# Modulation products of four column groups moved into the DeltaNet chain

## The chip, the cores and the metric

The kernel runs on one core of a Trainium2 chip. The metric is the device time of one execution in microseconds (us). Engines: TensorE (PE in the profile; its weight loads are PEld), VectorE (DVE), ScalarE (ACT), GpSimd (POOL) and SyncE (SP), whose queue here issues nearly all DMAs.

## The reference

One inference step of a hybrid backbone with two layers, over 512 latent tokens (`x_sample`) and 128 context tokens (`x_prompt`). Cut to what matters here:

```python
def trunk_layer(x, cond, ...):
    mod = (jax.nn.silu(cond) @ w_ada + b_ada)[:, None, :]
    shift1, scale1, gate1, shift2, scale2, gate2 = jnp.split(mod, 6, axis=-1)
    h = rmsnorm(x, norm1_g) * (1 + scale1) + shift1
    q, k, v, z, dn_a, dn_b, u_ssm, u_pool, gates = jnp.split(h @ w_in, offsets, axis=-1)
    o_dn, st_dn = deltanet_mixer(q, k, v, z, ...)      # chunked, in both directions
    o_ssm, st_re, st_im = s5_mixer(u_ssm, ...)         # complex diagonal scan, in both directions
    o_pool = pool_mixer(u_pool, pool_w, pool_scale)
    g_dn, g_ssm, g_pool = jnp.split(jax.nn.sigmoid(gates), N_BRANCH, axis=-1)
    merged = g_dn * (o_dn @ w_branch_dn) + g_ssm * (o_ssm @ w_branch_ssm) + g_pool * (o_pool @ w_branch_pool)
    x = x + gate1 * (merged @ w_out)
    h = rmsnorm(x, norm2_g) * (1 + scale2) + shift2
    x = x + gate2 * conv_ffn(h, ffn_w_up, ffn_conv, ffn_w_down)
```

`w_ada` is 1024 x 6144 in float32 for each layer; `cond` is one vector for the latent and one for the context tokens, so the modulation is a product of two rows with 25 MB of weights a layer. It depends on nothing but `cond`: it can be computed at any time before it is used.

## The kernel before

All activations stand transposed, 128 channels on the partitions and the 640 tokens along the free dimension, and a product of a weight tile with them (`mm3`, lines 377 to 389) is made of three float32r products, high and low parts, in two halves of 320 columns. Its accumulator is one of two `acc` tiles in PSUM. A weight tile is loaded by SP's queue into one of four raw buffers (`wraw`, tag of four), and split into a high part by ScalarE (L235) and a low part by VectorE (L372). Such a tile of 1024 input rows is 48 products, L384, L386 and L388.

**The modulation** is computed in column groups of 2048: group 0 is shift1 and scale1, group 1 gate1 and shift2, group 2 scale2 and gate2. `ada_pieces` gives a group as nine entries. Eight are pieces, one for each 128 rows of `w_ada`: two loads of 128 x 1024 (`wada`, L443), which take two of the same four raw buffers, and four products of 512 columns in 32-column tiles of the array (L446), which the profile counts as eight instructions. All eight pieces accumulate in one small PSUM tile; `sm` has four. The ninth entry transposes the row (L456) and adds the bias into `mods[l]`.

**The order of the work** comes from two sources. A layer runs, one after another: a state-space chain (`s5_chain`, with the branch that ends in the glu and `w_branch_ssm` tiles, here called the state-space output stretch), the DeltaNet chain, the projections, and the FFN. The chains are generators that yield an estimate of how much other work fits beside each step; a queue of other work, `Weave`, is stepped while it has credit from these estimates, times `wv.scale`. `extra` entries are put between the tiles of the queue; in the FFN, `ffn_extra` is called once a tile. The list that comes out so is then handed to a planner, which reorders the instructions of each engine by its own costs and readiness and takes the list order as priority, so that a later entry whose operands are there can be issued before an earlier one.

In the DeltaNet chain the queue holds the last four q/k/v tiles and the eight gate tiles (`gate`, stored to `g_dram`); `wv.drain(12)` runs it down to twelve entries ahead of the chain. The chain itself: `start` (transposes of K and V to DRAM), `ahead` and `dn_diag` (L1363, L1365, L1414), `dn_inverse` (L1463 to L1511), `dn_step` (L1552 to L1593), `finish` (L1876); nearly all of its products go to `sm` tiles, which VectorE or ScalarE read out. K, V and P are loaded back by SP's queue (L1532, L1533, L1542).

Group 0 of layer 0 is computed at the kernel's head by a function of its own. Group 1 of layer 0 stands among the tiles of the state-space chain of layer 0 and stays there. The other four groups stand as follows: group 2 of each layer among the tiles of its state-space output stretch, groups 0 and 1 of layer 1 in the FFN of layer 0.

Of the kernel before, what the change touches and what calls it, by code (L numbers as in the profile page):

```python
# [259 lines left out]
def hybrid_dit_kernel(ctx: ExitStack, tc: tile.TileContext, a, outs, depth=DEPTH, taps=None):  # L260
# [171 lines left out]
    def ada_pieces(l, p, mod, grp, E=None):  # L432

        box = {}

        def rows_k(k):
            if k == 0:
                box["ps"] = sm()
            ps = box["ps"]
            for hf in range(2):  # L440
                t = E() if E else wpool.tile([P, 1024], F32, name="wada", tag="wraw", bufs=WRAW)
                c0 = grp * 2048 + hf * 1024
                nc.sync.dma_start(t, a["w_ada"][l, k * P:(k + 1) * P, c0:c0 + 1024])  # L443
                for j in range(2):
                    q = 32 * (2 * hf + j)
                    PE.matmul(ps[q:q + 32, :], silu_c[:, k, :], t[:, j * 512:(j + 1) * 512],  # L446
                              start=k == 0, stop=k == KT - 1, tile_position=(0, q))
            if k == KT - 1:
                box["row"] = row = ar.take(512)
                S.activation(row.f, ps, AF.Copy)  # L450

        def finish():
            row = box["row"]
            pt = sm()
            for b in range(4):
                PE.transpose(pt[:, b * P:(b + 1) * P], row.f[:, b * P:(b + 1) * P], ident)  # L456
            row.free()

            src = pt.rearrange("p (b j r) -> p r j b", b=4, j=4)[:, 0:2]
            dst = mod[:, :, grp * 16:(grp + 1) * 16].rearrange("p s (j b) -> p s j b", j=4)  # L460
            bias = p["b_ada"][:, grp * 16:(grp + 1) * 16].rearrange("p (j b) -> p j b", j=4)
            for st in range(2):
                V.tensor_tensor(dst[:, st], src[:, st], bias, op=OP.add)

        return [(1.7, lambda k=k: rows_k(k)) for k in range(KT)] + [(0.6, finish)]
# [1165 lines left out]
        V.tensor_mul(y.f, y.f, sq.f)  # L1631
        sq.free()

    def layer(l, xs, p, qf, mod, wv, extra, ffn_extra, begin, nxt):

# [15 lines left out]
        def store(dr, i, t):  # L1653
            nc.sync.dma_start(dr[i], t.f)
            t.free()

        def gate(w):

            ps = acc()
            mm3(ps, w, hs)  # L1660
            g_ = ar.take(NT)
            S.activation(hv(g_.f), ps[:, :, :HF], AF.Tanh, scale=0.5)
            return g_

        def gate_w(n, m):
            return lambda: Stream(w_in, OFF_G + n * D, D).tile(m)
# [86 lines left out]
        def kq(m):  # L1753
            return tile_of(qkv, m, w_in, 0)
# [16 lines left out]
        extra = deque(extra)  # L1771
# [11 lines left out]
        work = [tile_of(glu, m, a["ssm_glu_w"][l], 0, 4) for m in range(4)]  # L1783
        for m in range(KT):
            work += gated(1, a["w_branch_ssm"][l], oS, m)
        extra.extend(ada_pieces(l, p, mod, 2))
        for w in work:
            wv.add(*w)
            if extra:
# [4 lines left out]
        qT, kT = ys[0:4], ys[4:8]  # L1794
        for m in range(8, 12):
            wv.add(*kq(m))
        for m in range(KT):
            wv.add(6.5, lambda w, m=m: store(g_dram, m, gate(w)), gate_w(0, m))
        wv.add(0.0, lambda: free_pairs(hb))


        def norms():
# [83 lines left out]
        tk = {}  # L1886
        with ln_exp():
            wv.run(together(deltanet_ab(l, hs, w_in, tk), norms()))
            wv.drain(12)
        vT = ys[8:12]  # L1890
        with tc.issue_after(last_rsq[0].ins):
            for t in vT:
                silu2(t)
        wv.run(one_by_one(start(), ahead(0, 3)))
        wv.run(together(inverse(0, 3), ahead(1, 2, 4)))
        wv.scale = 0.4
        wv.run(together(inverse(1, 2), inverse(4), steps((0, 0)), steps((1, 3))))
        wv.scale = 0.6
        wv.run(together(steps((0, 1), (0, 2), (0, 3)), steps((1, 2), (1, 1), (1, 0))))
        wv.scale = 1.0  # L1900
        wv.run(together(steps((0, 4)), steps((1, 4)), finish(2), finish(1)))
# [7 lines left out]
        first = []  # L1909
# [175 lines left out]
    wv = Weave(ar)  # L2085
    for l in range(depth):
        first = ada_pieces(0, ps_[0], mods[0], 1) if l == 0 else ()
        extra = deque()
        if l + 1 < depth:
            ps_.append({})  # L2090
            lps, lds = [], []
            kept = []
            extra.append(lambda: (kept.append(s5_kept()), lps.append(load_params(l + 1, GP))))
            extra.extend([lambda: None] * 4)
            extra.append(lambda: ps_[l + 1].update(params(l + 1, lps[0])))
            for grp in range(2):
                extra.extend(f for _, f in ada_pieces(l + 1, ps_[l + 1], mods[l + 1], grp))
            extra.extend([lambda: None] * (60 - len(extra)))
            extra.insert(60, lambda: lds.append(s5_load(l + 1, GP, kept[0])))
            extra.insert(64, lambda: qs.append(s5_params(lds[0])))  # L2100
        qf = (lambda: s5_params(ld0)) if l == 0 else lambda: qs[0]

        def nxt():
            w_in = a["w_in"][l + 1]
            ws = [wraw(w_in, OFF_SSM + m * P, KT, P) for m in range(2)]
            return scales(mods[l + 1], 8, ps_[l + 1]["norm1"]), mods[l + 1][:, :, 0:8], ws

        done = layer(l, xs, ps_[l], qf, mods[l], wv, first, extra, begin, nxt if l + 1 < depth else None)
        if done:
            xs, begin = done  # L2110

# [30 lines left out]
```

## Time and profile before

| | us |
|---|---|
| median of three runs | 2593.4 (2589.87 to 2594.01) |
| the profiled execution's own time | 2591.93 |
| its span, first to last instruction | 2590.2 |
| mean granted TensorE clock (1 is 2.4 GHz) | 0.973 |

| stretch, from the trace | us from the start |
|---|---|
| state-space output stretch, layer 0 / layer 1 | 390 to 520 / 1660 to 1790 |
| DeltaNet chain, layer 0 / layer 1 | 570 to 770 / 1830 to 2030 |
| FFN of layer 0 | 860 to 1330 |

The profile gives for each engine the time in which it was busy. A wait is put down to the instruction whose signal came last. Busy times of one engine in a stretch are compared with the length of the stretch: an engine that is busy all the time bounds it.

### The profile page before, as it was taken

The page shows a single profiled execution, that of the slowest core. Times are in us where ns is not written, and L with a number is a line of the kernel's source. Part 1 is how long each engine was busy: PE and PEld are TensorE (multiplying, and loading weights), DVE is VectorE, ACT ScalarE, POOL GpSimd, SP SyncE. Part 2 cuts the span into 40 slices and gives each one's busy share as a digit, 9 for nine tenths or more (in the row PEclk, how much of TensorE's full clock was granted, in tenths as well). Part 3 has the DMA queues.
Part 4 walks back from the last instruction along what each step waited for, and adds up shares of the span by engine and source line. Part 5 has one row for each costly group of instructions (what it writes and reads, how often), then busy time and mean ns, then how long its engine had stood idle before and what let it go on. Part 6 is the DMA issues. An engine that isn't in the chain of part 4 may idle for free. (4 is left out here: it accounts for less than half of the span.)

```text
span 2590.2 us, 43654 instructions
## 1 busy us (share of the span) xinstructions
PE 2440.7 (94%) x17225; PEld 2321.6 (90%) x17225; DVE 1608.3 (62%) x3250; ACT 989.8 (38%) x1792; POOL 555.2 (21%) x560
## 2 busy tenths in 40 slices
PE   7899989998889999999988999899989999999999
PEld 6688987997789988999988998799879899999998
DVE  5768863269866743553596687633897766445355
ACT  4242342363333531442443423424533354334243
POOL 3521320135342100000134404311445320000000
PEclk8899999999889999999999999999999999999999
DMA  9833327344253255322237232463454322222221
GB/s 309 162 112 94 91 64 233 114 127 140 94 178 95 74 172 178 98 67 81 75 115 103 59 113 79 118 197 99 138 166 160 112 66 74 74 74 78 78 66 66
DMA packets 382016, 297.29 MB, mean 115 GB/s; under 512 B 33706, under 2 KB 336500, under 8 KB 381812
## 3 DMA queue, kind: packets, MB, share of 16 engines
q1 hardware_dynamic: 377892, 286.53, 38.4%
q0 software_dynamic: 3552, 7.73, 1.2%
q8 instruction: 136, 2.23, 0.4%
q14 instruction: 68, 0.56, 0.1%
q10 hardware_dynamic: 368, 0.25, 0.0%
HBM read 251.45 MB, written 42.48 MB: 113 GB/s over the span
## 5 line engine op out<-in xcount | busy, mean ns | idle before, releaser
L384 PE MATMUL acc<-pg,whi 128*128 128x320 f32 x4064 | 943.2, 313 | 5.9 <-ACT pg L235 2.9
L388 PE MATMUL acc<-pg,wlo 128*128 128x320 f32 x4064 | 936.0, 311 | 8.0 <-DVE wlo L372 8.0
L386 PE MATMUL acc<-pg,whi 128*128 128x320 f32 x4064 | 938.0, 311 | 4.9 <-DVE pg L411 4.9
L372 DVE TENSOR_TENSOR wlo<-wraw,whi 128x512 fp32r<-128x512 f32 (+1 forms) x538 | 414.5, 776 | 524.3 <-ACT whi L235 518.1
L384 PEld LDWEIGHTS acc<-pg,whi 128*128 128x128 f32 x4064 | 681.4, 189 | 47.1 <-issue 16.7
L388 PEld LDWEIGHTS acc<-pg,wlo 128*128 128x128 f32 x4064 | 684.5, 189 | 10.5 <-DVE wlo L372 8.9
L386 PEld LDWEIGHTS acc<-pg,whi 128*128 128x128 f32 x4064 | 685.4, 189 | 6.0 <-DVE pg L411 5.4
L235 ACT ACTIVATE whi<-wraw 128x512 fp32r<-128x512 f32 (+1 forms) x538 | 331.7, 623 | 925.4 <-PE acc L386 723.0
L235 ACT ACTIVATE pg<-pg 128x640 f32<-128x640 f32 (+8 forms) x335 | 222.0, 682 | 262.5 <-DVE pg L1996 56.1
L235 ACT ACTIVATE pg<-sm 128x512 f32<-128x512 f32 (+9 forms) x245 | 109.5, 470 | 207.1 <-PE sm L1502 59.4
L235 ACT ACTIVATE pg<-acc 128x640 f32<-128x640 f32 (+3 forms) x196 | 127.0, 655 | 73.9 <-PE acc L388 49.5
L700 DVE SCALAR_TENSOR_TENSOR pg<-pg,cols_f 128x511 f32<-128x511 f32 (+1 forms) x130 | 65.9, 548 | 49.8 <-ACT pg L235 49.7
L411 DVE TENSOR_TENSOR pg<-pg,pg 128x640 fp32r<-128x640 f32 x84 | 68.6, 821 | 41.4 <-ACT pg L235 37.6
L713 POOL DMA_DIRECT2D pg<-in_ssm_lambda_re_dram x2 | 1.2, 583 | 407.9 <-ACT whi L235 407.9
L1685 POOL TENSOR_TENSOR pg<-pg,pg 128x640 f32<-128x640 f32 x21 | 38.9, 1855 | 226.1 <-DVE pg L1683 146.9
L691 DVE SCALAR_TENSOR_TENSOR pg<-acc,mod,pg 128x320 f32<-128x320 f32 x56 | 30.8, 549 | 78.3 <-PE acc L388 78.2
L235 ACT ACTIVATE pg<-acc,cols_f 128x640 f32<-128x640 f32 (+1 forms) x88 | 68.3, 776 | 0.0
L701 DVE SCALAR_TENSOR_TENSOR pg<-pg,cols_h 128x511 f32<-128x511 f32 (+1 forms) x130 | 65.6, 546 | 0.0
L446 PE MATMUL sm<-wada,silu_c 128*32 128x512 f32 x320 | 57.9, 627 | 8.0 <-DMA wada<-in_w_ada_dram 8.0
L1683 DVE SCALAR_TENSOR_TENSOR pg<-pg,acc 128x640 f32<-128x640 f32 x48 | 39.0, 817 | 40.9 <-PE acc L388 35.3
L906 POOL TENSOR_TENSOR pg<-pg,pg 128x512 f32<-128x512 f32 (+1 forms) x32 | 54.7, 1710 | 1.9
L901 POOL TENSOR_TENSOR pg<-s_cp,pg 128x640 f32<-128x640 f32 x16 | 27.6, 1725 | 127.4 <-PE acc L388 55.8
(392 smaller groups left out, 2960.8 us busy)
## 6 DMA issues: line engine op xcount, KB each, us to landing
wraw<-in_w_in_dram SPq DMA_DIRECT2D x96, 512.0 KB, 4.4
wraw<-in_ffn_w_up_dram SPq DMA_DIRECT2D x88, 512.0 KB, 3.9
wada<-in_w_ada_dram SPq DMA_DIRECT2D x80, 512.0 KB, 4.4
wraw<-in_ffn_w_down_dram SPq DMA_DIRECT2D x32, 512.0 KB, 3.9
mg_dram<-pg SPq DMA_DIRECT2D x32, 320.0 KB, 2.2
pg<-mg_dram SPq DMA_DIRECT2D x32, 320.0 KB, 5.2
wraw<-in_w_out_dram SPq DMA_DIRECT2D x16, 512.0 KB, 3.9
pg<-in_w_ada_dram SPq DMA_DIRECT2D x6, 1024.0 KB, 10.8
```

The lines of the kernel that those rows point to most:

```text
L235: ins = self.engine.activation(out, in_, func, **kw)
L372: V.tensor_sub(lo, src, hi)
L384: PE.matmul(ps[:M, h, :HF], hi[:, k, :M], hh[:, h * HF:(h + 1) * HF], start=first and k == 0, stop=False)
L386: PE.matmul(ps[:M, h, :HF], hi[:, k, :M], hl[:, h * HF:(h + 1) * HF], start=False, stop=False)
L388: PE.matmul(ps[:M, h, :HF], lo[:, k, :M], hh[:, h * HF:(h + 1) * HF], start=False, stop=last and k == n - 1)
L411: V.tensor_sub(lo.r, src, hi.r)
L446: PE.matmul(ps[q:q + 32, :], silu_c[:, k, :], t[:, j * 512:(j + 1) * 512], start=k == 0, stop=k == KT - 1, tile_position=(0, q))
L700: V.scalar_tensor_tensor(y[:, b + 1:e], r[:, b:e - 1], w0, y[:, b + 1:e], op0=OP.mult, op1=OP.add)
L701: V.scalar_tensor_tensor(y[:, b:e - 1], r[:, b + 1:e], w2, y[:, b:e - 1], op0=OP.mult, op1=OP.add)
L906: E.tensor_tensor(oo, oo, t.f, op=OP.add if r else OP.subtract)
L1683: V.scalar_tensor_tensor(hv(g_.f), hv(g_.f), 1.0, ps[:, :, :HF], op0=OP.add, op1=OP.mult)
L1685: GP.tensor_tensor(g_.f, g_.f, mg.f, op=OP.add)
```

## The change

The four groups leave their places and become entries of the queue of the DeltaNet chain, between the gate tiles: three entries behind the first, two behind each of the others, the rest behind the eighth. Layer 0's chain gets group 2 of layer 0, the parameter transposes of layer 1 and group 0 of layer 1; layer 1's chain gets groups 2 and 1 of layer 1. The loads of layer 1's parameters go from the FFN of layer 0 to its state-space chain in the list. `drain` runs the queue down to the number of entries that were added from the gates on, and two of the chain's scales are raised, 0.4 to 0.5 and 0.6 to 0.75. Nothing that is computed changes.

```diff
--- before.py
+++ after.py
@@ -1631,7 +1631,7 @@
         V.tensor_mul(y.f, y.f, sq.f)
         sq.free()
 
-    def layer(l, xs, p, qf, mod, wv, extra, ffn_extra, begin, nxt):
+    def layer(l, xs, p, qf, mod, wv, extra, late, ffn_extra, begin, nxt):
 
 
 
@@ -1783,7 +1783,6 @@
         work = [tile_of(glu, m, a["ssm_glu_w"][l], 0, 4) for m in range(4)]
         for m in range(KT):
             work += gated(1, a["w_branch_ssm"][l], oS, m)
-        extra.extend(ada_pieces(l, p, mod, 2))
         for w in work:
             wv.add(*w)
             if extra:
@@ -1794,9 +1793,17 @@
         qT, kT = ys[0:4], ys[4:8]
         for m in range(8, 12):
             wv.add(*kq(m))
+        before = len(wv.q)
+        late = deque([*ada_pieces(l, p, mod, 2), *late])
         for m in range(KT):
             wv.add(6.5, lambda w, m=m: store(g_dram, m, gate(w)), gate_w(0, m))
+            for _ in range(2 if m else 3):
+                if late:
+                    wv.add(*late.popleft())
         wv.add(0.0, lambda: free_pairs(hb))
+        for w in late:
+            wv.add(*w)
+        after_v = len(wv.q) - before
 
 
         def norms():
@@ -1886,16 +1893,16 @@
         tk = {}
         with ln_exp():
             wv.run(together(deltanet_ab(l, hs, w_in, tk), norms()))
-            wv.drain(12)
+            wv.drain(after_v)
         vT = ys[8:12]
         with tc.issue_after(last_rsq[0].ins):
             for t in vT:
                 silu2(t)
         wv.run(one_by_one(start(), ahead(0, 3)))
         wv.run(together(inverse(0, 3), ahead(1, 2, 4)))
-        wv.scale = 0.4
+        wv.scale = 0.5
         wv.run(together(inverse(1, 2), inverse(4), steps((0, 0)), steps((1, 3))))
-        wv.scale = 0.6
+        wv.scale = 0.75
         wv.run(together(steps((0, 1), (0, 2), (0, 3)), steps((1, 2), (1, 1), (1, 0))))
         wv.scale = 1.0
         wv.run(together(steps((0, 4)), steps((1, 4)), finish(2), finish(1)))
@@ -2085,16 +2092,16 @@
     wv = Weave(ar)
     for l in range(depth):
         first = ada_pieces(0, ps_[0], mods[0], 1) if l == 0 else ()
+        late = ada_pieces(l, ps_[l], mods[l], 1) if l else []
         extra = deque()
         if l + 1 < depth:
             ps_.append({})
             lps, lds = [], []
             kept = []
-            extra.append(lambda: (kept.append(s5_kept()), lps.append(load_params(l + 1, GP))))
-            extra.extend([lambda: None] * 4)
-            extra.append(lambda: ps_[l + 1].update(params(l + 1, lps[0])))
-            for grp in range(2):
-                extra.extend(f for _, f in ada_pieces(l + 1, ps_[l + 1], mods[l + 1], grp))
+            first = [*first, (0.0, lambda: lps.append(load_params(l + 1, GP)))]
+            late.append((0.6, lambda: ps_[l + 1].update(params(l + 1, lps[0]))))
+            late.extend(ada_pieces(l + 1, ps_[l + 1], mods[l + 1], 0))
+            extra.append(lambda: kept.append(s5_kept()))
             extra.extend([lambda: None] * (60 - len(extra)))
             extra.insert(60, lambda: lds.append(s5_load(l + 1, GP, kept[0])))
             extra.insert(64, lambda: qs.append(s5_params(lds[0])))
@@ -2105,7 +2112,7 @@
             ws = [wraw(w_in, OFF_SSM + m * P, KT, P) for m in range(2)]
             return scales(mods[l + 1], 8, ps_[l + 1]["norm1"]), mods[l + 1][:, :, 0:8], ws
 
-        done = layer(l, xs, ps_[l], qf, mods[l], wv, first, extra, begin, nxt if l + 1 < depth else None)
+        done = layer(l, xs, ps_[l], qf, mods[l], wv, first, late, extra, begin, nxt if l + 1 < depth else None)
         if done:
             xs, begin = done
 
```

## Rows read from the trace of the kernel before

**Rows 1.** The page: engines' busy time (share) and TensorE's forty slices, in tenths.

```profile
PE 2440.7 (94%) x17225; PEld 2321.6 (90%) x17225; DVE 1608.3 (62%) x3250; ACT 989.8 (38%) x1792; POOL 555.2 (21%) x560
...
PE   7899989998889999999988999899989999999999
```

**Rows 2.** Busy time by stretch, all engines; columns in the first line.

```profile
core 0: us, PE busy (x) PEld busy (x) DVE busy (x) ACT busy (x) POOL busy (x), PEclk, DMA share, GB/s
390.00:450.00 60.00, 60.00 (x366) 45.96 (x365) 20.67 (x32) 17.31 (x28) 3.13 (x2) 1.00 0.75 240
570.00:645.00 75.00, 64.60 (x433) 62.97 (x431) 69.80 (x117) 29.48 (x60) 39.06 (x34) 0.93 0.44 140
645.00:770.00 125.00, 104.79 (x813) 97.20 (x814) 92.57 (x198) 41.53 (x107) 52.92 (x44) 0.88 0.41 135
940.00:1040.00 100.00, 100.00 (x684) 88.63 (x683) 39.80 (x79) 27.00 (x45) 0.00 (x0) 1.00 0.61 182
1830.00:1930.00 100.00, 87.84 (x594) 84.92 (x594) 91.24 (x163) 47.61 (x102) 45.71 (x41) 0.95 0.49 155
1930.00:2030.00 100.00, 88.23 (x791) 82.66 (x790) 79.32 (x164) 34.99 (x85) 51.27 (x42) 1.00 0.46 157
```

**Rows 3.** Timeline of TensorE, FFN of layer 0: start us, length us, what.

```profile
941.08 0.46 PE L386 MATMUL acc<-pg,whi 128*128 128x320 f32 x2
941.38 0.46 PE L388 MATMUL acc<-pg,wlo 128*128 128x320 f32 x2
941.77 1.06 PE L446 MATMUL sm<-wada,silu_c 128*32 128x512 f32 x8
...
943.16 0.46 PE L386 MATMUL acc<-pg,whi 128*128 128x320 f32 x2
...
966.10 0.46 PE L388 MATMUL acc<-pg,wlo 128*128 128x320 f32 x2
966.40 0.60 PE L456 MATMUL sm<-cst,pg 128*128 128x128 f32 x4
...
967.13 0.46 PE L386 MATMUL acc<-pg,whi 128*128 128x320 f32 x2
```

**Rows 4.** Timeline of TensorE, output stretch of layer 0: half a piece.

```profile
408.91 1.05 PE L446 MATMUL sm<-wada,silu_c 128*32 128x512 f32 x4
```

**Rows 5.** Busy time of line 446 alone, output stretches of layers 0 and 1.

```profile
390.00:450.00 60.00, 14.55 (x64) 2.12 (x64) 1.00 0.75 240
1660.00:1725.00 65.00, 12.88 (x64) 1.84 (x64) 0.95 0.67 213
```

**Rows 6.** Timeline of TensorE and VectorE, head of layer 1's output stretch.

```profile
1663.70 1.92 PE L446 MATMUL sm<-wada,silu_c 128*32 128x512 f32 x16
1669.45 1.92 PE L446 MATMUL sm<-wada,silu_c 128*32 128x512 f32 x4 [3.83 <-DMA wada<-in_w_ada_dram]
1671.64 1.92 PE L446 MATMUL sm<-wada,silu_c 128*32 128x512 f32 x4 [0.26 <-DMA wada<-in_w_ada_dram]
1673.49 0.64 PE L384 MATMUL acc<-pg,whi 128*128 128x320 f32 x1
...
1668.15 0.69 DVE L372 TENSOR_TENSOR wlo<-wraw,whi 128x512 fp32r<-128x512 f32 x1 [0.80 <-ACT whi L235]
```

**Rows 7.** TensorE's waits, chain of layer 0: total us, times, longest us.

```profile
PE sm L1463 <- DVE pg L1457: 9.1, 3, 6.4
PE sm L1414 <- ACT pg L235: 7.5, 3, 3.3
PE acc L405 <- ACT pg L235: 4.4, 2, 4.2
```

**Rows 8.** Instructions of line 317, the parameter loads; first and last start last.

```profile
L317 POOL DMA_DIRECT2D rows_a<-in_b_ada_dram x1: 535/535/535, 61.0 to 61.0; - x1
```

**Rows 9.** Waits of SP's queue, chain of layer 0: total us, times, longest us.

```profile
SPq L359 <- DVE pg L1428: 17.5, 2, 12.5
SPq L1532 <- DVE pg L1427: 14.8, 1, 14.8
```

## The prediction

> **What bounds the kernel now.** I read the page first: TensorE is busy 94% of the span, and the slices show where it is not, in the stretches that hold the DeltaNet chain and in those that hold the start of the state-space scan; the FFN slices stand at 9 throughout [rows 1]. Then the busy times by stage. In the FFN of layer 0 (940 to 1040 us) TensorE is busy for all of 100 us, and in the state-space output stretch of layer 0 (390 to 450 us) for all of 60: there every product that is taken out shortens the kernel by its own length. In the DeltaNet chain of layer 0 (570 to 770 us) TensorE stands still for 75 - 64.60 = 10.4 and 125 - 104.79 = 20.2 us, in that of layer 1 (1830 to 2030 us) for 12.2 and 11.8 us: 54.6 us in all. VectorE is the busier engine in the first part of each chain (69.80 of 75, 91.24 of 100), and the granted clock falls to 0.88 in one part, a mixture of 1.2 and 2.4 GHz [rows 2]. So the kernel is bound by TensorE outside the chains, and inside them by a mixture of TensorE and the chain's own hand-overs to VectorE and ScalarE. The change carries TensorE work from the first kind of place to the second. The median of the three runs shown is 2593.4 us, the profiled execution took 2591.93; the sum is made against the latter, and 1.5 us are added at its end.
>
> **What is taken out.** A column group is eight pieces (two loads of 512 KB each, products at L446) and a closing step (four transposes, L456). In the FFN a piece is one burst of eight products of 1.06 us. Pairs of ordinary products follow each other there every 0.30 us; from the pair before the burst to the second pair behind it pass 943.16 - 941.38 = 1.78 us, of which two pairs would have taken 0.59: a piece costs 1.19 us. A closing step costs 967.13 - 966.10 - 0.59 = 0.44 us [rows 3]. Two groups leave the FFN: 16 x 1.19 + 2 x 0.44 = 19.9 us.
>
> One group leaves the output stretch of layer 0. There the two loads of a piece landed apart and its products ran as two bursts of 1.05 us [rows 4], so the same 64 instructions took 14.55 us [rows 5]. With 0.13 us at the edges of some 13 bursts, and the closing step, that is 14.55 + 1.7 + 0.44 = 16.7 us.
>
> One group leaves that of layer 1, where its products took 12.88 us [rows 5]. Three bursts of 1.92 us stand at its head and wait for their loads, once for 3.83 us; the ordinary products start behind them at 1673.49. Their weights had been split by 1668.15 + 0.69 = 1668.84, so the head costs 4.6 us, not its whole length [rows 6]. The rest, 12.88 - 5.76 = 7.12 us, stands among ordinary products: with 1.0 us at the edges and the closing step 8.6 us. Together 13.2 us. All that is taken out: 19.9 + 16.7 + 13.2 = 49.8 us.
>
> **What is put in.** Each chain gets two groups. If every piece runs as one burst, a chain gets 16 x 1.19 + 2 x 0.44 = 19.9 us of TensorE; if every piece falls into two bursts, 16 x 2.38 + 0.88 = 39.0. The transfers of the chain are light (DMA share 0.41 to 0.49, against 0.75 where the pieces split and 0.61 in the FFN where they did not) [rows 2], so I take a quarter of the pieces split: 16 x 1.19 x 1.25 + 0.88 = 24.7 us, for both chains 49.4 (bounds 39.8 and 78.0).
>
> How much of it falls into standing time? A piece has its operands when its two loads have landed, and needs neither VectorE nor ScalarE, so it can run while the chain waits for these. But a piece holds two of the four raw weight buffers, so that at most two pieces, 2.4 us, lie ready for one gap. The chain of layer 0 has a gap of 6.4, one of 4.2 and one of 3.3 us among many of 1 to 2 [rows 7]; with each cut at 2.4 and those below 1.2 left out, about half of the 30.6 us can be used. I take half for both chains: 27.3 us hidden (bounds none and 39.8, all that the lower count puts in).
>
> The eight gate tiles are pushed back by the pieces between them. By the queue's own costs (6.5 a gate, 1.7 a piece, 0.6 a closing step) it holds 81 where it held 52; the chain's steps with the new scales give 14 + 18.4 + 3.3 + 5.4 + 9 + 9 + 9 = 68, so the last gate and the four to five entries behind it are written behind the last chain step. I cost this at nothing: the list order is only a preference of the planner (the loads of layer 1's parameters stand in the FFN in the code, and ran at 61.0 us [rows 8]), and TensorE waits there for ScalarE's and VectorE's eviction, splitting and gating anyway (4.4 us at L405 [rows 7]). Without that cover it costs the four or five pieces, 6 us a layer. In exchange fewer weight splittings fall on VectorE while it is at its busiest. The parameter loads that change their place cost nothing for the same reason, and the three small transposes with them move at the same price.
>
> On SP's queue 32 issues a chain are new. An issue that waits for a raw buffer holds up what is queued behind it: the loads of K, V and P that the steps need. The queue already waits up to 12.5 us for one weight buffer and 14.8 us for a place for a V load [rows 9]; these were issued well ahead of their use. What is late next, if a piece is late, is the V or K load of the step after, and then GpSimd's scaling of it. I cost it at nothing in the sum and leave it to the upper bound.
>
> Sum: -49.8 + 49.4 - 27.3 = -27.7 us; 2591.93 - 27.7 = 2564.2, and with 1.5 for the median 2566 us. With the bounds of the three costs: from -49.8 (everything in one burst and hidden) to +28.2 (everything in two bursts, nothing hidden).
>
> **The rivals.**
>
> *Hidden whole, chance 0.15.* Standing time of 24.0 us or more in each chain is more than the 19.9 us that unsplit pieces need, so the chains need not grow at all: 2593.4 - 49.8 = 2543.6. For it speaks that VectorE, not TensorE, is at its limit in the first parts [rows 2]; against it the two-piece stock. A further gain lies in the clock: a granted mean of 0.93, 0.88 and 0.95 over busy times of 64.60, 104.79 and 87.84 us [rows 2] is 4.5 + 12.6 + 4.4 = 21.5 us lost to the lower level; filled gaps could give back half, which leads to 2533. The Trainium skill ("TensorE: Matmul & The Clock Gate", HAM oscillation) says that waits between bursts let the clock fall, so that the next burst runs at half rate; by that rule the filling would pay twice. The granted clock of these rows agrees as far as it is low where TensorE stood still; that more work raises it no run shows yet.
>
> *Nothing hidden, chance 0.15.* The chain keeps its own pace, each piece delays the chain product behind it by its length, and the pieces split as in layer 0's output stretch. Then the chains give back 49.4 to 78.0 us against 49.8: 2593 to 2622, with 2597 the middle of what I hold likely. For it: TensorE is already busy for 84 to 88% of the chains.
>
> *A small accumulator too few, chance 0.13: slower.* A group accumulates in one of the four small PSUM tiles (`sm`) from its first piece to its last. With two groups in a row the chain, which uses these tiles for nearly all of its products, has three for most of its length. If the turnover of these tiles set its pace all the time, 200 us would become 267; the gain of 27.7 us is used up at 13.9 us a chain, 7%. I price the rival at 10%, 20 us a chain: 2566 + 40 = 2606. For it: TensorE's longest waits in the chain are at products into `sm`, 9.1 us behind VectorE and 7.5 behind ScalarE [rows 7]. Against it: these name an operand's producer as well as a tile's reader, and with VectorE at its limit a slower feed costs nothing until VectorE runs dry. The Trainium skill ("Perfetto Trace Analysis", Matmuls) wants independent groups of products to rotate through different PSUM banks, so that one is read out while the next is filled; a bank pinned for a chain's length goes against that, and by this rule alone the time is the 2606 of this rival. Which of the two binds, no row of before can show.
>
> **How the numbers follow.** The forecast, half hidden, has 0.55; the rivals 0.15, 0.15 and 0.13; 0.02 is left for a stall at SP. The forecast's own range is 2550 to 2582 (hidden 12 to 40 us). The 8-in-10 range reaches from 2540, which leaves out half of the first rival, to 2605, which leaves out about half of the last: 0.15 outside. About 0.2%, 5 us, is what a measurement of this kernel can tell from no change. Faster: 0.55 + 0.15 + 0.04 of the second rival = 0.74. Same: 0.06 of the second and 0.02 of the third, 0.08. Slower: 0.18.
>
> **What would show it.** In the changed kernel no L446 instruction stands in the FFN of layer 0 and in both output stretches, and the stretches are shorter by 20, 17 and 13 us. In the chains 128 such instructions each; their busy time near 17 to 20 us a chain says that most ran as one burst, 30 that they split. The two chains together should be longer by 20 to 25 us with TensorE's standing time down by about 27; chains of the old length mean the first rival, longer by 45 or more the second. Chains that grow by more than the pieces' own time, with TensorE's standing time no smaller and its waits at `sm` products longer, mean the third. The prediction is wrong if the output stretches do not shrink because something else there ends just as late.

## The result and the profile after

The changed kernel takes 2637.8 us (median of four runs, 2636.1 to 2640.7) against 2593.7 for the kernel before on the same chip: a ratio of 1.0174, interval 1.0157 to 1.0192. It is slower by 44 us where 28 less were forecast. The profiled execution took 2636.1, its span 2634.0.

The page of the changed kernel, its TensorE row and TensorE's slices (against [rows 1]):

```profile
PE 2443.4 (93%) x17225; PEld 2316.8 (88%) x17225; DVE 1597.5 (61%) x3250; ACT 1008.7 (38%) x1804; POOL 551.2 (21%) x560
...
PE   7899899969989999999988999897898899999998
```

The same products, the same busy time; the span grew by standing time. To see where, I cut both traces at the same products: the last token transposes of the state-space chain (L1012), the first products of the gate logits that open the DeltaNet stage (L1272), the last step product (L1593) and the first product of the stage behind (L519). Length of each stretch in us, worked out from the timelines; the last two columns are experiments told below (e11 is the kernel before with four rows stored elsewhere, e10 the change with no cost in the queue and the buffers as before):

| stretch | before | after | e11 | e10 |
|---|---|---|---|---|
| head to the output stretch, layer 0 | 381.2 | 379.7 | 379.1 | 378.8 |
| output stretch, layer 0 | 123.3 | 106.6 | 123.3 | 106.6 |
| DeltaNet stage to its last step, layer 0 | 241.5 | 237.9 | 244.4 | 260.1 |
| the rest of that stage, layer 0 | 84.1 | 117.3 | 82.1 | 83.1 |
| FFN, layer 0 | 497.5 | 477.2 | 498.1 | 477.4 |
| state-space chain, layer 1 | 336.2 | 349.8 | 349.0 | 339.6 |
| output stretch, layer 1 | 117.3 | 96.6 | 119.0 | 104.5 |
| DeltaNet stage to its last step, layer 1 | 227.9 | 250.2 | 252.1 | 263.9 |
| the rest of that stage, layer 1 | 79.2 | 120.5 | 79.2 | 77.9 |
| FFN, layer 1, and end | 502.0 | 498.3 | 499.3 | 499.3 |

After against before: taken out 16.7 + 20.3 + 20.7 = 57.7; the two DeltaNet stages longer by 29.6 + 63.6 = 93.2; layer 1's state-space chain, which the change does not touch, by 13.6; head and end -5.2. Together, from unrounded lengths, +43.8.

Busy time by stretch of the kernel before, columns as in [rows 2]: for layer 0 from the first K/V transposes to the diagonal inverse (L1414), from there to the last step, and the whole DeltaNet stage; for layer 1 the whole stage:

```profile
530.90:585.84 54.94, 50.74 (x347) 48.29 (x345) 36.12 (x59) 31.63 (x53) 19.56 (x18) 1.00 0.47 152
585.84:745.94 160.10, 139.27 (x1066) 131.78 (x1067) 130.73 (x261) 53.57 (x128) 75.74 (x65) 0.90 0.41 133
504.47:830.05 325.58, 292.08 (x2102) 276.62 (x2102) 237.40 (x434) 134.51 (x269) 123.46 (x103) 0.94 0.42 132
...
1781.08:2088.16 307.08, 280.66 (x2102) 266.21 (x2102) 237.84 (x434) 133.86 (x269) 125.31 (x103) 0.98 0.44 140
```

The same of the changed kernel, with the rest of the stage behind the last step as a third line in layer 0:

```profile
512.73:564.39 51.66, 34.49 (x235) 32.00 (x233) 31.48 (x52) 26.80 (x45) 19.63 (x19) 0.87 0.39 129
564.39:724.24 159.85, 145.83 (x1150) 127.87 (x1150) 127.86 (x265) 54.87 (x130) 74.45 (x64) 0.98 0.52 163
724.24:841.50 117.26, 105.49 (x669) 92.28 (x666) 63.68 (x94) 39.10 (x69) 27.32 (x19) 0.93 0.64 204
486.31:841.50 355.19, 310.78 (x2242) 273.08 (x2241) 235.21 (x444) 137.45 (x272) 124.52 (x105) 0.95 0.53 168
...
1765.03:2135.71 370.68, 318.43 (x2238) 278.52 (x2238) 232.75 (x441) 150.49 (x282) 123.37 (x101) 0.93 0.51 161
```

Standing time is length less TensorE's busy time. It was to fall by 27; it went from 33.5 + 26.4 = 59.9 to 44.4 + 52.3 = 96.7 us. Behind the diagonal inverse it did fall (20.8 to 14.0 in layer 0), but ahead of it it rose from 4.2 to 17.2, and the gates and pieces left behind the last step made that part 33 us longer. TensorE's waits in layer 0's stage, columns as in [rows 7]:

```profile
PE sm L1414 <- DVE pg L1413: 16.2, 1, 16.2
PE acc L384 <- ACT whi L235: 10.0, 3, 5.4
PE sm L446 <- DMA wada<-in_w_ada_dram: 5.1, 2, 3.4
```

The several waits at L1463, L1414 and L405 have mostly become a single one at the diagonal inverse, and two kinds are new: a gate's weights not yet split, a piece's loads not yet landed. The timelines of SP's queue and of TensorE show what was loaded meanwhile:

```profile
522.75 0.35 SPq L443 DMA_DIRECT2D wada<-in_w_ada_dram  x1
571.60 0.38 SPq L359 DMA_DIRECT2D wraw<-in_w_in_dram  x1
```

```profile
564.39 6.19 PE L1414 MATMUL sm<-pg,cst 128*128 128x240 f32 x30 [16.25 <-DVE pg L1413]
570.51 1.92 PE L446 MATMUL sm<-wada,silu_c 128*32 128x512 f32 x16
```

Two pieces were loaded by about 528 (the page has a median of 5.4 us from issue to landing), held all four raw buffers, and ran only behind the diagonal inverse, at 570.51; no gate weight was loaded between 522.75 and 571.60, while TensorE stood for 16.25 us.

### The profile page after: what moved, and what is told of

Same layout as the page of the kernel before. It is cut to its first block, busy times and chain, and to the rows that moved or that the text cites. A ratio compares the mean times of both kernels' runs of the same rounds, so it can differ in the third digit from the quotient of the medians.

```text
span 2634.0 us, 43670 instructions
## 1 busy us (share of the span) xinstructions
PE 2443.4 (93%) x17225; PEld 2316.8 (88%) x17225; DVE 1597.5 (61%) x3250; ACT 1008.7 (38%) x1804; POOL 551.2 (21%) x560
## 5 line engine op out<-in xcount | busy, mean ns | idle before, releaser
L384 PE MATMUL acc<-pg,whi 128*128 128x320 f32 x4064 | 943.1, 313 | 21.0 <-ACT whi L235 14.4
L384 PEld LDWEIGHTS acc<-pg,whi 128*128 128x128 f32 x4064 | 682.6, 189 | 47.0 <-ACT whi L235 21.3
L372 DVE TENSOR_TENSOR wlo<-wraw,whi 128x512 fp32r<-128x512 f32 (+1 forms) x538 | 402.2, 752 | 503.8 <-ACT whi L235 481.2
L235 ACT ACTIVATE pg<-pg 128x640 f32<-128x640 f32 (+8 forms) x335 | 221.7, 682 | 267.5 <-DVE pg L2003 62.4
L1685 POOL TENSOR_TENSOR pg<-pg,pg 128x640 f32<-128x640 f32 x24 | 47.0, 1959 | 237.6 <-DVE pg L1683 234.7
L446 PE MATMUL sm<-wada,silu_c 128*32 128x512 f32 x320 | 66.4, 663 | 14.0 <-DMA wada<-in_w_ada_dram 14.0
L700 DVE SCALAR_TENSOR_TENSOR pg<-pg,cols_f,pg 128x511 f32<-128x511 f32 x86 | 43.4, 548 | 31.9 <-ACT pg L235 31.9
L700 DVE SCALAR_TENSOR_TENSOR pg<-pg,cols_f 128x511 f32<-128x511 f32 x90 | 45.6, 548 | 27.0 <-ACT pg L235 27.0
L1414 PE MATMUL sm<-pg,cst 128*128 128x240 f32 (+24 forms) x120 | 24.4, 359 | 37.7 <-ACT pg L235 21.4
## 6 DMA issues: line engine op xcount, KB each, us to landing
pg<-in_w_ada_dram SPq DMA_DIRECT2D x6, 1024.0 KB, 10.9
```

Of the source, the lines that this page charges most:

```text
L235: ins = self.engine.activation(out, in_, func, **kw)
L372: V.tensor_sub(lo, src, hi)
L384: PE.matmul(ps[:M, h, :HF], hi[:, k, :M], hh[:, h * HF:(h + 1) * HF], start=first and k == 0, stop=False)
L700: V.scalar_tensor_tensor(y[:, b + 1:e], r[:, b:e - 1], w0, y[:, b + 1:e], op0=OP.mult, op1=OP.add)
L1685: GP.tensor_tensor(g_.f, g_.f, mg.f, op=OP.add)
```

## The experiments

Single runs are given with the run of the kernel before on the same chip in brackets, kernels timed several times with their ratio to it and its interval. Over all its runs the kernel before took 2584.1 to 2599.9 us, so a few us between single runs tell nothing.

**Does the work or the queue cost the time? Raw buffers, PSUM tile, order of the gates.** Four kernels. e1: the four groups left out of the changed kernel, empty entries in their places.

```diff
     def ada_pieces(l, p, mod, grp, E=None):
+        if (l, grp) != (0, 1):
+            return [(1.7, lambda: None)] * KT + [(0.6, lambda: V.memset(mod[:, :, grp * 16:(grp + 1) * 16], 0.1))]
```

> The changed kernel with the four moved groups left out: their loads, products and transposes are gone (the modulation values are set to a constant), the queue keeps empty entries of the same costs. It measures what the pieces themselves cost where they stand now, against what the altered queue costs. If the pieces cost the 93 us by which the two chains grew (starved gates, waits behind the chain), the time is about 2545 us. If the later places of the gate tiles and the raised scales cost a good part of it, the gates still stand behind the chain and the time stays above 2565.

2584.4 [2591.0]. With none of the moved work the kernel gains only 7 us: the output stretches and the FFN are shorter by 16.7, 18.6 and 21.3, but the DeltaNet stages are longer by 19.0 and 23.3 and layer 1's state-space chain by 14.4, 57 us without a single piece. The pieces then cost 2637.8 - 2584.4 = 53 us, about all of their 49.4 (the two kernels also place their buffers differently, see below). There are two losses to explain, not one.

e2: the moved groups load into buffers of the page store (`ar`, the common store of the activations) instead of the four raw buffers.

```diff
-                t = E() if E else wpool.tile([P, 1024], F32, name="wada", tag="wraw", bufs=WRAW)
+                own = ar.take(1024) if (l, grp) != (0, 1) else None
+                t = own.f if own else wpool.tile([P, 1024], F32, name="wada", tag="wraw", bufs=WRAW)
```

> The changed kernel, but the loads of the four moved groups go to buffers of the page store instead of the four raw weight buffers that they share with the gate tiles. Theory 1 (raw buffers): two pieces take all four buffers before the chain starts and cannot run before the chain gives up a small PSUM tile, so no gate weight can be loaded and TensorE stands still for 16 and 21 us at the heads of the two chains, and the gates that did not run there run behind the chain; then the holes go to below 5 us each and the time falls by 35 us or more, to about 2595 or less. Theory 2 (one small PSUM tile too few for the chain): the tile is held as long as before, the time stays within 10 us of 2637.

2642.6 [2591.0]: no gain. TensorE's standing time ahead of the diagonal inverse did fall, from 17.2 and 22.2 us to 9.6 and 5.3, but in the two stages together it stayed, 96.6 against 96.7. This edit moves other buffers too (below), so it prices the raw buffers only together with that.

e3, and the same kernel timed several times as e13: the kernel before, to hold one small PSUM tile through each chain.

```diff
+        pin = sm()
+        PE.matmul(pin[:, :P], ident, ident, start=True, stop=True)
         wv.run(one_by_one(start(), ahead(0, 3)))
...
+        pout = small("pin_out", 4)
+        V.tensor_copy(pout, pin[:, 0:4])
         with ln_exp():
             wv.run(finish(0))
```

> The kernel before, with one of the four small PSUM tiles held from the start of each DeltaNet chain to its last part (one product into it at the start, one copy out at the end) and no piece moved. Theory 2 (a tile too few): each chain grows by 20 us or more, the time is above 2630. Theory 1 (raw buffers): the chain lives with three tiles, below 2605.

> The kernel before with one small accumulator held through the chain (2583.1 us in one look), all its work done, with a product into it ahead of the chain and one copy out of it behind; its buffers lie as in the kernel before. If the 8 us were the planner's other order and hold: a ratio of 0.995 to 0.998. If they were the spread of single looks: 0.998 to 1.002.

2583.1 [2591.0] in one run, 0.9999 (0.9986 to 1.0013) in e13; the 8 us of the single run were spread. But neither kernel held the tile. The copy out of it stands behind the chain in the list, and the planner put it ahead of the chain. TensorE and VectorE in e13, layer 0:

```profile
529.83 0.39 PE L1895 MATMUL sm<-cst 128*128 128x128 f32 x2
531.06 0.15 DVE L1926 COPY pin_out<-sm 128x4 f32<-128x4 f32 x1
```

The tile was free again 1.4 us after its product began, 54 us ahead of the diagonal inverse at 585.19 (layer 1: 1806.68 and 1807.99, the inverse at 1856.05; e3 alike). The chain had its four tiles, and what three would cost was not measured.

e4: all eight gates ahead of the pieces.

```diff
-            for _ in range(2 if m else 3):
-                if late:
-                    wv.add(*late.popleft())
```

> The changed kernel with all eight gate tiles ahead of the moved pieces in the queue. Theory 1: the gates find their raw buffers free and fill the heads of the chains as in the kernel before, so both holes go; the pieces run late, in the steps and behind the chain, where each costs its products and a part of its load: about 2600 to 2615. Theory 2: the small tile is held for the later part of the chain only, where the steps need it most; the time stays above 2625.

2660.0 [2591.0]: the pieces pile up behind the last step, which makes that part 42.2 and 51.6 us longer. Buffers move in this kernel too.

**What a kernel without the groups takes.** e5: they are left out of the kernel before, in place (the edit of e1, on the kernel before). e6: e1 with a look-ahead for weights over up to five entries in the queue's `step`. e7: the changed kernel with its work whole, the moved entries at no cost in the chain, the scales as before. e8: the kernel before with one group moved, group 2 of layer 1 from its output stretch to the FFN of layer 0.

```diff
             wv.drain(after_v)
+            wv.q = deque((c if w_ else 0.0, f, w_) for c, f, w_ in wv.q)
...
-        wv.scale = 0.5
+        wv.scale = 0.4
...
-        wv.scale = 0.75
+        wv.scale = 0.6
```

> The kernel before with the same four groups left out where they stood (modulation values set to a constant, empty entries of the same costs). It is the counterpart of the changed kernel without them (2584.4 us): the difference is what the altered queue alone costs. Theory Q (the queue: pieces between the gates push the gates back and cut the look-ahead that loads and splits a gate's weights a tile early): about 2541 us, so that the queue costs some 43. Theory W (the pieces were cheap where they stood): 2570 or more.

> The changed kernel with the four groups left out, and the queue's look-ahead mended: when an entry is run, the weights of the next tile are requested even if up to five entries without weights stand between. If the lost look-ahead is what the altered queue costs, the time falls from 2584 to about 2545. If the later places of the gates cost it, it stays within 10 us of 2584.

> The changed kernel with all its pieces, but in the DeltaNet chain entries without weights cost nothing and the two scales are those of before, 0.4 and 0.6: the gates come at the credits of before, and the pieces with them. Theory Q by places: nothing is left for behind the chain, the tails shrink by 25 us or more each, the time is 2600 or less. If the pieces' own products and loads are what costs, the waits move to the front of the chains and the time stays above 2620.

> The kernel before with one group moved the other way: group 2 of layer 1 goes from that layer's state-space output stretch to the FFN of layer 0, behind groups 0 and 1. By the changed kernel's trace the output stretch gets 13 to 20 us shorter without it, and by the FFN's rows the group costs 10 us there as whole bursts: the time falls by 3 to 10 us, to 2581 to 2588. If a stretch of layer 1 gives the gain back, as the state-space stretch did with 14 us in the changed kernel, the time is 2590 or more.

All [2595.7]. e5 2571.5: 24 us gained where the parts taken out are worth 49.8; layer 1's state-space chain and DeltaNet stage grew by 9.2 and 18.1 though nothing in them changed but the places of buffers and the planner's order. e6 2584.1, as e1: look-ahead is not it. e7 2623.7, where theory Q had 2600 or less: the parts behind the last step are back at their old length, 35 and 40 us shorter than in the changed kernel, but the parts ahead of it are 29 and 24 longer, and on balance 14 us of the loss are gone. e8 2612.1: that move was to gain 3 to 10 and lost 16; FFN +12.5, output stretch -17.2 as their own rows say, and again layer 1's state-space chain and DeltaNet stage +9.5 and +24.4. In e1, e5 and e8 these two grow though no work was added to them.

**The places of buffers.** The page store gives a buffer its place when the program is built, by what came back when. A group's row takes a place there for its closing step; where that take goes, later buffers lie elsewhere. Following the store's rule through both programs, 1050 of 1371 buffers lie elsewhere in the changed kernel, none in e3. e9: e5 with an empty take and return where each row's was. e11: the kernel before, its work whole, with the four rows in a small buffer of their own: 991 of the other 1367 buffers move. e10: e7 with both edits, so that those 1367 lie as in the kernel before; e12 is e10 timed several times. By the same rule e1, e2, e4 to e8 and e16 move buffers too, 724 (e8) to 1071 (e4) of them, and e7 places 1017 otherwise than the changed kernel: their times hold a price of places that they don't show apart. e9, e10, e12 to e15, e17 and e18 move none.

```diff
-                box["row"] = row = ar.take(512)
+                box["row"] = row = small("ada_row", 512) if (l, grp) != (0, 1) else ar.take(512)
...
+    def places():
+        kept = []
+        return ([(1.7, lambda: None)] * (KT - 1) + [(1.7, lambda: kept.append(ar.take(512)))]
+                + [(0.6, lambda: kept[0].free())])
```

> The kernel before with the work of the four groups left out where it stands (the modulation values are a constant), as in the run before that also left them out in place (span 2569.7), with one difference: each group's row still takes its place in the page store and gives it back, so that every other buffer lies where it lies in the kernel before. Theory P (placement): in the earlier run layer 1's state-space stretch grew by 9 us and its DeltaNet stage by 18 because the buffers came to lie otherwise. Then here the state-space stretch of layer 1 is 336 +- 3 us, its DeltaNet stage 307 +- 4, and the time 2541 to 2547. Rival C (the planner's order, or the clock after the shorter FFN): placement is nothing, both stretches stay long, time 2565 to 2575.

> The kernel before with all its work in its old place; the one edit is that the rows of the four groups lie in a small buffer of their own and take nothing from the page store. Theory P: layer 1's state-space stretch and DeltaNet stage grow as they did without the groups, by 9 and 18 us, so 2610 to 2622. Rival C: no different from the kernel before, 2585 to 2600.

> The changed kernel with the moved entries at no cost in the chain (as in the run of 2623.7), and with each moved group's row in a small buffer of its own while an empty take and return of the page store stands at each group's old place, so that the other buffers lie as in the kernel before. All the work is done. By theory P with the full price of the moved work (24 and 29 us in the two chains, as against the run without the groups): 2542 + 53 = 2595, between 2588 and 2602, no gain and no loss. If a part of the work were hidden once the placement is kept: below 2585. Rival C: about as the run without this, 2615 to 2630.

> The kernel of the run of 2593.2 us once more, all its work done, timed in rounds against the kernel before: pieces in the chain, entries without weights at no cost, buffers where they lie in the kernel before. Theory 'nothing hidden, placement the rest': the moved work costs in the chain what it saved outside, so a ratio to the kernel before between 0.996 and 1.004. If any tenth of the moved 50 us were hidden and stays so: 0.996 or less. Rival (placement was luck of that one look): above 1.006.

e9 2555.8 [2596.5]: e5 was 26 us short of its 49.8, e9 is 9 short, so placement is part of it but, without the groups, not all: the 2541 to 2547 were missed. e11 2627.4 [2596.5]: +31 us with no work moved at all, more than the 2610 to 2622 that theory P gave it. e10 2593.2 [2596.5], and in e12 2590.3 with a ratio of 0.9992 (0.9982 to 1.0003): with the places and the queue's costs kept, the change is worth nothing. The planner also lists the work otherwise when the places change; whether its order or the places themselves cost the time, no run separates. Layer 1's DeltaNet stage in e11, and TensorE's longest wait in it up to the last step:

```profile
1795.02:2126.28 331.26, 289.33 (x2102) 273.50 (x2102) 233.41 (x431) 134.86 (x269) 128.40 (x103) 0.94 0.41 130
```

```profile
PE sm L1417 <- ACT pg L235: 17.6, 2, 12.5
```

L1417 there is L1414 of the kernel before, whose waits in this stretch are 2.3 us in three. The stage does the same 2102 products in 24.2 us more: 15.5 more standing, and 8.7 more busy at a granted clock of 0.94 against 0.98.

**Where the pieces of e10 went.** Its windows, layer 0 to and from the diagonal inverse and whole, layer 1 whole:

```profile
511.86:564.14 52.28, 34.47 (x235) 31.96 (x233) 31.25 (x52) 26.60 (x45) 18.53 (x18) 0.89 0.36 122
564.14:745.57 181.43, 172.70 (x1313) 145.60 (x1314) 136.22 (x276) 59.75 (x138) 75.81 (x65) 0.98 0.69 221
485.43:828.70 343.27, 308.85 (x2241) 273.72 (x2241) 238.46 (x444) 135.66 (x271) 122.48 (x103) 0.96 0.55 174
...
1750.28:2092.06 341.78, 313.74 (x2238) 278.30 (x2238) 239.28 (x441) 136.62 (x271) 123.34 (x103) 0.95 0.55 175
```

Behind the diagonal inverse the pieces do fill: TensorE stands 8.7 us there against 20.8. Ahead of it 17.8 against 4.2. The second gate, stored 73 us after the stage's start in the kernel before, is stored at 103. e14 and e15 put the first piece behind the second and the third gate, with the rest spread three and four to a gate; e16 is the edit of e14 on the changed kernel.

```diff
-            for _ in range(2 if m else 3):
+            for _ in range(3 if m else 0):
```

> The kernel of the run of 2590.3 us (pieces in the chain at no cost, buffers as before), with one edit: no piece is queued between the first and the second gate, three instead of two behind each later one; all the work is done. Theory G (the second gate's place): in the changed kernels the gate that TensorE multiplied ahead of the diagonal inverse in the kernel before (stored 73 us after the stage's start) comes behind three pieces and is stored at 103, so TensorE stands 17.3 and 14.3 us ahead of the diagonal inverse where it stood 4.2 and 4.2; the pieces do fill standing time behind it (20.8 and 15.5 down to 7.1 and 10.3). With the second gate back, it stands some 4 to 8 us there, the fill stays, and the time is 2565 to 2580. Rival H (nothing can be hidden, the standing time only moves): 2586 to 2596.

> As the run with two gates ahead of the first piece, with three gates ahead, and four pieces behind each later one. Theory G: the second gate is ahead of the diagonal inverse here too, so 2565 to 2582; the fewer gates are left between the pieces, the nearer they stand together, so 0 to 8 us more than with two. Rival H: 2586 to 2600.

> The changed kernel itself (costs, scales and buffers as changed) with the one edit that no piece is queued between the first and the second gate and three behind each later one. Theory G: TensorE's standing time ahead of the diagonal inverse falls from 17.2 and 22.2 us to 4 to 10, so 2605 to 2625, unless the buffers' places, which this moves too, take it back. Rival H: 2630 to 2645.

e14 1.0048 (1.0031 to 1.0065), e15 1.0058 (1.0039 to 1.0076), e16 2648.7 [2593.0]. The gate came back ahead (stored at 72 in e14) and the wait there shrank, to 10.9 and 6.4 us in layer 0, but the standing time behind rose to 14.8 and 25.5. All three are slower than either of their two theories allowed. TensorE's waits in e15, layer 0, behind the start of the diagonal inverse:

```profile
PE sm L1471 <- DVE pg L1465: 21.4, 2, 21.1
PE sm L451 <- DMA wada<-in_w_ada_dram: 3.7, 3, 2.3
```

L1471 is L1463 before, the first products of the next part. The same hole stands one part later, where now the pieces are: theory G falls.

e17 and e18 list two and three pieces ahead of the diagonal inverse and put its first product behind theirs.

```diff
     def dn_diag(chunks, st, ac):
+        for _ in range(2 if seen["first"] else 0):
+            if seen["wv"].q[0][2] is None:
+                seen["wv"].step()
...
-            PE.matmul(ps[:, at:at + n], bd16, t.f, start=True, stop=True)
+            ahead_of = seen["ins"][-1:] if seen["first"] else []
+            seen["first"] = False
+            with tc.issue_after(ahead_of[0].ins) if ahead_of else nullcontext():
+                PE.matmul(ps[:, at:at + n], bd16, t.f, start=True, stop=True)
```

> The kernel of the run of 2590.3 us with one edit: the first two pieces of each chain are listed ahead of the diagonal inverse, and its first product is put behind theirs in TensorE's order; all the work is done. In that run the two pieces' four loads were issued at 502 to 524 us and all four raw buffers were theirs, TensorE stood 16.41 us at 548.8 to 565.18 ahead of the diagonal inverse, and their products, ready all the while, ran behind it at 571.11; the next weight load was issued at 572.20. Theory J (order: a ready product behind a waiting one on TensorE can't fill its wait, and the buffers it holds keep the gates out): their products run ahead of 550, the next weight loads are issued some 30 to 40 us earlier, and the time falls by 4 us (the two pieces of each chain alone) to 25 us (the second gate too): 2565 to 2587. Rival H (the standing time only moves): 2587 to 2597, with the products moved all the same.

> As the run with two pieces listed ahead of the diagonal inverse, with three. Theory J: one piece more a chain in the wait, and the second gate's weights are next at the raw buffers: 2 to 6 us less than with two, 2560 to 2585. Rival H: 2587 to 2600.

1.0024 (1.0013 to 1.0034) and 1.0003 (0.9993 to 1.0012). The products did not run ahead of 550. The timeline of TensorE in e17, layer 0:

```profile
553.20 3.64 PE L453 MATMUL sm<-wada,silu_c 128*32 128x512 f32 x16 [5.55 <-DVE pg L1388]
```

They now wait for a VectorE operation of the chain, and it is one that reads an `sm` tile out:

```profile
552.46 0.69 DVE L1388 TENSOR_TENSOR pg<-sm,pg 128x512 f32<-128x512 f32 x1
```

The product starts 0.05 us after its end: a group's first piece needs a free tile, not its loads alone. The second gate came to 94 us from 103, the next weight load from 572.2 to 555.5, and the stage was no shorter (347.3 us against 343.3 in e10). No edit of the order paid for itself. No version beat the kernel before.

## Why the prediction was wrong

**What is taken out: right.** Layer 0's output stretch 16.7 us as forecast, the FFN 20.3 against 19.9, layer 1's output stretch 12.8 in e10 against 13.2 (20.7 in the changed kernel, but its state-space chain gave 13.6 back).

**What is put in: right in size.** The pieces' own products (L446, L451 in e10) took 24.7 and 25.4 us in the two stages of e10 (26.9 and 26.9 in the changed kernel), where the sum had 24.7 with the closing steps. TensorE is busy 16.8 + 33.1 = 49.9 us longer in these stages of e10, against 49.4; in the changed kernel 18.7 + 37.8 = 56.5. The pieces don't account for 16.8 and 33.1 being so far apart; the granted clock moved with it: that of the stage went from 0.94 to 0.96 in layer 0 and from 0.98 to 0.95 in layer 1.

**Half hidden, 27.3 us: the step that failed.** Its argument is that a piece needs no more than its loads and so can run while the chain waits. Both halves fail in the traces. A group's first piece needs a free `sm` tile as well, and in e17 it waited 5.55 us for VectorE to read one out. And in the changed kernel two loaded pieces stood behind the waiting chain product in TensorE's list: in its trace the products start in the order of the program's list, which is fixed before the run. In e10, at no cost in the queue and with the places kept, standing time is 34.4 + 28.0 against 33.5 + 26.4 us: nothing hidden, by e12's interval to within some 5 us. The stretch behind the diagonal inverse was filled, the one ahead lost its gate. Of the rivals "nothing hidden" (2593 to 2622) comes nearest to e12's 2590.3; e12 is not the changed kernel, whose 2637.8 lie above every rival. The cause stays open at one point: why the standing time of both stages doesn't fall below the old 59.9 us by more than 4.3, however the pieces are listed (62.4 in e10, 65.4 in e14, 73.9 in e15, 55.6 in e17, 60.1 in e18, from windows like those above). Neither the second gate's place nor the order at the first wait is the whole of it, and the tile that the pieces take from the chain is an untested candidate.

**Costs taken as nothing, two of them wrong.** Queue places: e7 takes 14 us less than the changed kernel. By size that is near the "6 us a layer without cover", and the cover was not there (TensorE's waits behind the last step in layer 0 are for a gate's weights, 5.4 us, and a piece's loads, 5.1). But the two DeltaNet stages are shorter by 5.6 and 16.5 us, and the edit of the queue moves 1017 buffers, so how much of the 14 us is the queue is not shown. Placement: it was not in the sum at all. e11 prices it at 31 us; e7 less e10, which differ in the rows' places alone, at 30; without the groups, e5 less e9, it was 16. The changed kernel's loss of 44 us is 14 (to e7), 30 (from there to e10) and nothing (from there to the kernel before): differences of one row of kernels, which add up by themselves. Against the forecast the miss is 72 us: the 27.3 that were not hidden, and 14.1 and 30.5 for what stood at nothing.

**The rivals.** The PSUM tile stays untested, as e3 and e13 did not hold it. The changed kernel shows the sign that the prediction gave for it, stages longer than the pieces' own time and the longest wait at a product into `sm`, but e11 shows that sign with no piece in the chain (17.6 us at the same product). e2 and e4 came out where their texts had put this theory, but both move buffers. That a tile too few costs 40 us is not borne out: in e10 the two groups of layer 0 held one from 570.8 to 616.6 and from 658.7 to 718.1, and the time was that of the kernel before. Whether the rule of the Trainium skill that stood beside it ("Perfetto Trace Analysis", Matmuls: rotate independent groups through PSUM banks) binds here, no run shows. SP's queue: its issues of piece loads waited 23.9 us in layer 0 for products of pieces to free a buffer; e2 gave the loads other buffers, kept such waits (28.1 us) and was no faster, but moved buffers, so what they cost by themselves stays open.

## What to carry to other kernels

Filling an engine's waits needs at least the filler ahead of the waiting instruction in that engine's list, a free tile for its result, and buffers not taken from the filler that was there; here even e17 and e18, which listed it ahead, gained nothing. A sum of gaps in the trace is not a saving. Where a program places its buffers by history and a planner orders it, a small edit upstream can move everything behind it: test that first with an edit that moves only the places (here +31 us with no work moved), and compare a change with the places kept. An experiment that is to hold something must be read in its trace before its time is: e13's tile was free after 1.4 us. A work item that leaves a full engine for one that is busy 90% should be priced at its full length until a run shows less.

## What the runs showed of the hardware

The same 16 instructions of two pieces took 1.92 us in the changed kernel (570.51), behind 6 us of the diagonal inverse's products, and 3.64 in e17 (553.20), directly behind a wait of 5.55 us. Busy time and granted clock of the two stretches, columns as in [rows 2] (the clock is the third from the right):

```profile
570.51:572.43 1.92, 1.92 (x18) 0.48 (x17) 1.77 (x3) 0.30 (x2) 1.41 (x2) 1.00 0.48 128
553.20:556.84 3.64, 3.64 (x16) 0.59 (x16) 3.60 (x5) 0.00 (x0) 2.55 (x2) 0.50 0.24 73
```

The granted clock is 1.00 (2.4 GHz) in the one and 0.50 (1.2 GHz) in the other. Standing time ahead of filler so makes the filler dear. The Trainium skill ("TensorE: Matmul & The Clock Gate", HAM oscillation) says that a burst behind a long wait runs at half rate; the rows agree. It bears on the rival "hidden whole", which gave half of the lost clock back: the granted clock of layer 0's DeltaNet stage went from 0.94 to 0.95 in the changed kernel and that of layer 1 from 0.98 to 0.93. As the standing time did not fall there, whether filled gaps raise the clock no run shows.
